# A hybrid RWKV-7 / HGRN2 block: two transposes moved from TensorE to VectorE and DMA, HGRN2 units overlapped, TensorE's durations re-estimated

## The chip, the cores and the metric

The kernel runs on one core of a Trainium2 chip, as one program in one launch. The metric is the device time of one execution in microseconds; the median of several executions is compared. All data are float32. Five engines work side by side, each on its own queue of instructions in order: TensorE (PE, with its weight load PEld), VectorE (DVE), ScalarE (ACT), GpSimd (POOL) and SyncE (SP), which here only issues DMAs. ScalarE issues some DMAs too. TensorE writes to PSUM; the other data lie in SBUF (128 partitions) or in DRAM.

## The reference, cut to what matters

One layer of a trunk block over 1024 tokens of width 1024. The change touches the first third, the token mixing:

```python
u = rmsnorm(h, norm_mix_g)
cols = u @ w_in                       # [RWKV-7 columns | HGRN2 columns | gate_a | gate_b]
y_a = rwkv7_branch(rw_cols, ...)      # 16 heads of 64: a delta-rule state per head, GroupNorm, bonus, gate g
y_b = hgrn2_branch(hg_cols, ...)      # 8 heads of 128: gated linear recurrence in chunks of 64 tokens
h = h + (sigmoid(gate_a) * y_a + sigmoid(gate_b) * y_b) @ w_out
# then cross-attention into 256 memory tokens, a SwiGLU feed-forward layer, a last RMSNorm
```

RWKV-7, per token: `state = state * w + (state @ a) b^T + v k^T`, `o = state @ r`; then GroupNorm per head, `* ln_w + ln_b`, plus a bonus term, times a gate g. HGRN2, per chunk of 64 tokens: `b = cumsum(log f)`, `scores[t,s] = sum_k q[t,k] exp(b[t,k] - b[s,k]) k[s,k]` for s up to t, `o = scores @ i + (q exp(b)) @ state`, and the state is carried on.

## The kernel before

**Stages.** `rw_prep` (up to about 400 us) projects the RWKV-7 columns and writes the chunk factors AR, BK, V and the gate g to DRAM. `mixing` (400 to 1300 us) runs the RWKV-7 recurrence, the HGRN2 branch, the rest of the projection and the merge. Attention and the feed-forward layer follow. Only `mixing` and the planner class `Pace` change.

**The order in mixing.** The order of all engines' instructions is fixed at build time by a planner. Every piece of work is a generator (`job`, `bkt`, `values`, `merge`, `hgrn`, `level`, `blocks`, `state`, `ev_*`, `weights`, ...). It yields the engine it wants next, the tiles that must be ready, the room that must be free in a ring of buffers, a condition and a priority. `Pace` keeps a clock for each engine, and `Pace.note` adds an estimated duration for each instruction; `Pace.matmul` (L172 to L184) estimates TensorE's: something for a change of form (`took`, L177), 0.109 for a transpose, `0.0155 + 0.000417 * cols` for a float32r product, and by columns for a float32 one (L184). The loop at L1615 resumes what is due by these clocks. TensorE's default work is `project()`: 768 steps ("slots") of three matmuls of 512 columns, the HGRN2 and gate columns of w_in, float32 split in two float32r halves. Between two other pieces of work at least RUN = 3 slots are put, if any are due. The estimates set only the order; on the chip engines wait by semaphores.

**RWKV-7 jobs.** There are 16 jobs (`job(n)`), one for 8 heads and 128 tokens, two chunks of 64, one each PERIOD = 41 slots at the earliest. Job n loads AR and BK (128 partitions x 8 x 128), multiplies them (psc), inverts a triangular matrix in blocks of 16 and 32 (Aq, Tq, UD, pu, py) and then does two steps of the recurrence: `cm<-Z,AR`, R, `cm<-R,U`, Z, `cm<-Z,BKT`, `po<-Z,SR`. `bkt(n, BK)` (L836) makes BKT, in which each of BK's eight 128x128 blocks is transposed: two groups of four TensorE transposes into PSUM (pbk), each copied to SBUF by ScalarE. BK's buffer is free (`locks.remove("BK")`) after the second. After the recurrence, the job normalizes po into xc (128 tokens-in-chunk and head parity x 8 x 64), multiplies by ln_w, adds zb (ln_b and bonus, from DRAM), and writes xc to `yad`, tokens by features, in four DMAs of 64 KB with runs of 256 bytes (L1090 to L1094).

**The merge.** When four jobs have written a half of the tokens and the gates are there, `merge(j, h)` (L1131) loads one 128-feature strip of yad by tokens (mya, in `tok3` order), turns it with four TensorE transposes (pya), multiplies it on VectorE by sigmoid(gate_a) * g (msa, from DRAM) and adds the HGRN2 side (msb), and the sum goes to y_d. For the last strip, j = 7, `last_gates` (L1289) does the product ahead (gya). `turned` counts strips turned; the key projections of attention, at the end of `project()`, wait until all 16 are (L1583).

**HGRN2 units.** `hgrn(j, h)` (L1424) is one head and 512 tokens, 16 in all. It starts when the unit before has issued its output (`hstate["done"]`, L1426), then starts `blocks` (factors within 4 tokens), `level` for 8, 16 and later 32 and 4, and `state` (L1376: eb, kh, qe, pkh, pSh, and the chain of states Sh). TensorE makes scores psB, psA, psl, which VectorE merges into one tile `sc`, and then the output poh. The flag "free" is set when the last level's factors reach TensorE (L1470).

Of the kernel before, what the change touches and what calls it, by code (L numbers as in the profile page):

```python
# [10 lines left out]
F32 = mybir.dt.float32  # L11
# [21 lines left out]
class Pace:  # L33
# [138 lines left out]
    def matmul(self, aps, op):  # L172
# [4 lines left out]
        took = 0.11 if form != self.form else 0.0  # L177
# [6 lines left out]
        return took + max(0.02, 0.00173 * cols / min(2 if rows == outs == 64 else 4, 128 // rows * 128 // outs))  # L184
# [3 lines left out]
def tile_trunk(ctx, tc, x, mem, norm_mix_g, w_in, rw_mu, rw_w0, rw_w2, rw_a0, rw_a2, rw_g2,  # L188
# [153 lines left out]
    def scratch(name, shape):  # L342
        return dram.tile(shape, F32, name=name)
# [7 lines left out]
    yad = scratch("ya_d", [S, D])  # L351
# [380 lines left out]
    def mixing(mctx):  # L732
# [50 lines left out]
        def pe(*tiles, **kw):  # L783
            return on("PE", *tiles, **kw)
# [51 lines left out]
        def bkt(n, BK):  # L836

            BKT = BKTs[n] = jp.tile([P, 8, P], F32, tag="BKT", name="BKT")
            for q in range(2):
                yield pe(BK, room=W1)  # L840
                pbk = pw.tile([P, 4, P], F32, tag="w", name="pbk")
                for e in range(4):
                    nc.tensor.transpose(pbk[:, e, :], BK[:, 4 * q + e, :], ident)
                pace.hold(pbk)
                yield on("ACT", pbk, prio=-1)
                nc.scalar.activation(BKT[:, 4 * q:4 * q + 4, :], pbk, AF.Copy)
                pace.drop(pbk)
            locks.remove("BK")

# [7 lines left out]
        def job(n):  # L857
# [146 lines left out]
            for c in range(2):  # L1004
# [31 lines left out]
                yield pe(Z, BKTs[n], prio=-2, cond=lambda: c == 0 or last or n + 1 in states)  # L1036
# [51 lines left out]
            nc.gpsimd.tensor_tensor(xf, xf, zb, op=ALU.add)  # L1088
            locks.remove("zb")
            yield on("SP", xc)  # L1090
            ys = yad[i * P:(i + 1) * P, j0 * P:(j0 + 4) * P].rearrange("(c t) (j q v) -> q c t j v", c=2, j=4, q=2)
            for hh in range(2):
                for c in range(2):
                    nc.sync.dma_start(out=ys[hh, c], in_=x4[H[hh], :, c, :])  # L1094
# [17 lines left out]
        turned = [0]  # L1112
# [18 lines left out]
        def merge(j, h):  # L1131
# [20 lines left out]
            ya = t(0, [P, 4, P], "mya")  # L1152
            nc.sync.dma_start(out=ya, in_=tok3(yad, h, j * P, P))
# [3 lines left out]
            yield pe(ya, room=W1, prio=1)  # L1157
            pt = pw.tile([P, 4, P], F32, tag="w", name="pya")
            for i in range(4):
                nc.tensor.transpose(pt[:, i, :], ya[:, i, :], ident)  # L1160
            pace.drop(ya)
            turned[0] += 1
            if pool is fp:
                locks.discard("zb")
            pace.hold(pt)
            yield on("DVE", pt, y, prio=-1)
            nc.vector.tensor_tensor(y, pt.rearrange("p i t -> p (i t)"), y, op=ALU.mult)
            pace.drop(pt)
# [120 lines left out]
        def last_gates():  # L1289
# [5 lines left out]
            ya = [jp.tile([P, 4, P], F32, tag="BS", name="mya") for _ in range(NHALF)]  # L1295
            nc.sync.dma_start(out=g, in_=gd[j].rearrange("h p t -> p h t"))
            for h in range(NHALF):
                nc.sync.dma_start(out=ya[h], in_=tok3(yad, h, j * P, P))
            for h in range(NHALF):
                yield pe(ya[h], room=W1, prio=1)  # L1300
                pt = pace.hold(pw.tile([P, 4, P], F32, tag="w", name="pya"))
                for i in range(4):
                    nc.tensor.transpose(pt[:, i, :], ya[h][:, i, :], ident)
                yield on("DVE", pt, g, prio=-1)
                nc.vector.tensor_tensor(g[:, h, :], pt.rearrange("p i t -> p (i t)"), g[:, h, :], op=ALU.mult)
                pace.drop(pt)
                flags.add(("gya", h))
                turned[0] += 1
# [67 lines left out]
        def state(j, h, M):  # L1376
# [8 lines left out]
            yield on("POOL", eb, q)  # L1385
# [38 lines left out]
        def hgrn(j, h):  # L1424

            yield pe(cond=lambda: hstate.get("done", 0) == NHALF * j + h  # L1426
# [918 lines left out]
```

## Time and profile before

| | us |
|---|---|
| median of 3 runs | 2315.07 (2314.65 to 2315.83) |
| profiled execution | 2322.77 |
| its span, first to last instruction | 2321.1 |

| mixing stage, instructions by group | count | mean ns |
|---|---|---|
| TensorE pbk<-ident,BK (transposes) | 128 | 281 |
| TensorE pya<-ident,mya (transposes) | 64 | 277 |
| ScalarE BKT<-pbk, 128x512 | 32 | 595 |
| VectorE msa<-pya,msa, 128x512 | 14 | 690 |
| VectorE UD<-TD, 32x32 transposes of 128x256 | 16 | 446 |

A group's mean is the time of one instruction from start to end. TensorE's instructions overlap in its pipeline, so means and busy times of TensorE are larger than the time from one start to the next. Idle time of an engine counts only where the engine sets the pace. "A <- B" in a wait list: an instruction of tile A waited for one that writes or reads tile B. PEclk is the share of TensorE's clock that was granted.

### The profile page before, as it was taken

How to read it: one execution, taken by the hardware profiler on the slowest of the kernel's cores; microseconds unless marked ns; L12 is line 12 of the kernel's file. 1: busy time of each engine (PE TensorE's matmuls, PEld its weight loads, DVE VectorE, ACT ScalarE, POOL GpSimd, SP SyncE). 2: the span in 40 equal slices, each digit the busy share in tenths (PEclk: the TensorE clock that was granted, in tenths of full speed). 3: DMA queues.
4: the chain of work that ended last, by engine and by line, in shares of the span. 5: the costliest groups of instructions: out<-in, count | busy, mean ns of one | idle time of the engine just before them, and what ended most of it. 6: DMA issues, size and time to landing. Idle time of an engine off the chain costs nothing.

```text
span 2321.1 us, 46517 instructions
## 1 busy us (share of the span) xinstructions
PE 2266.5 (98%) x18006; PEld 1845.9 (80%) x18006; DVE 1528.3 (66%) x2510; ACT 1134.9 (49%) x2214; POOL 1027.7 (44%) x1109
## 2 busy tenths in 40 slices
PE   7999999999999999999999999999999999999998
PEld 5788887778878877778787788888878888888887
DVE  5788884656676766875757466555768675566655
ACT  6545454465666655556665424443453333334533
POOL 3655555554565655665656100000266655551212
PEclk9999999999999999999999999999999999999999
DMA  5444445334435345445333897117933423248653
GB/s 173 124 128 125 126 125 172 76 89 98 99 95 135 81 107 130 126 97 128 90 98 102 279 353 261 55 55 267 287 112 118 129 91 117 93 160 303 206 173 118
DMA packets 424666, 331.06 MB, mean 143 GB/s; under 512 B 140619, under 2 KB 349629, under 8 KB 423037
## 3 DMA queue, kind: packets, MB, share of 16 engines
q1 hardware_dynamic: 353405, 313.93, 44.1%
q10 hardware_dynamic: 69696, 9.44, 2.8%
q0 software_dynamic: 1344, 4.72, 0.5%
q8 instruction: 142, 2.33, 0.4%
q14 instruction: 79, 0.65, 0.1%
HBM read 228.12 MB, written 99.35 MB: 141 GB/s over the span
## 4 chain that ended last, share of the span: by engine, by line
PE 69%; DMA 5%; DVE 4%; POOL 3%; issue 2%; ACT 2%; SPq 0%; ACTq 0%; POOLq 0%; DVEq 0%
PE pproj L103 19%; PE P L304 6%; PE P L303 6%; PE P L305 6%; PE acc L304 3%; PE acc L305 2%; PE acc L303 2%; PE cm L103 2%; PE pw L305 2%; PE pw L303 2%; PE pw L304 2%; PE poh L103 1%; PE pq L304 1%; PE pq L303 1%; PE pq L305 1%
## 5 line engine op out<-in xcount | busy, mean ns | idle before, releaser
L103 PE MATMUL pproj<-uh,whi 128*128 128x512 f32 x768 | 321.8, 419 | 3.7 <-ACT sa L103 1.4
L103 PE MATMUL pproj<-ul,whi 128*128 128x512 f32 x768 | 302.7, 394 | 1.8 <-issue 1.8
L103 PE MATMUL pproj<-uh,wlo 128*128 128x512 f32 x768 | 302.6, 394 | 0.0
L289 POOL TENSOR_TENSOR wl<-wraw,wh 128x512 fp32r<-128x512 f32 x87 | 120.6, 1392 | 204.8 <-ACT wh L285 171.6
L303 PE MATMUL pproj<-uh,whi 128*128 128x512 f32 (+1 forms) x432 | 177.5, 411 | 1.0 <-ACT uh L331 0.7
L285 ACT ACTIVATE whi<-wraw 128x512 fp32r<-128x512 f32 (+1 forms) x166 | 100.9, 618 | 158.4 <-PE pw L305 73.7
L103 POOL TENSOR_TENSOR wlo<-wraw,whi 128x512 fp32r<-128x512 f32 x96 | 129.3, 1355 | 105.3 <-ACT whi L103 95.5
L103 PEld LDWEIGHTS pproj<-uh,whi 128*128 128x128 f32 x768 | 145.3, 189 | 38.3 <-DVE q L103 2.0
L103 PEld LDWEIGHTS pproj<-ul,whi 128*128 128x128 f32 x768 | 145.4, 189 | 35.0 <-issue 2.2
L305 PE MATMUL pproj<-uh,wlo 128*128 128x512 f32 (+1 forms) x432 | 170.4, 394 | 1.8 <-POOL wlo L289 1.8
L304 PE MATMUL pproj<-ul,whi 128*128 128x512 f32 (+1 forms) x432 | 170.4, 395 | 0.0
L103 PEld LDWEIGHTS pproj<-uh,wlo 128*128 128x128 f32 x768 | 145.8, 190 | 24.9
L280 POOL TENSOR_TENSOR ss<-ss,nhalf 128x4 f32<-128x4 f32 (+1 forms) x7 | 6.2, 883 | 324.6 <-DVE ss L279 205.6
L103 ACT ACT_TABLE_LOAD x102 | 130.9, 1283 | 18.5 <-issue 6.0
L289 POOL TENSOR_TENSOR wlT<-wraw,whT 128x512 fp32r<-128x512 f32 x72 | 101.0, 1412 | 84.9 <-ACT whT L285 67.0
L285 ACT ACTIVATE wh<-wraw 128x512 fp32r<-128x512 f32 x143 | 87.1, 624 | 97.0 <-PE P L304 69.0
L289 DVE TENSOR_TENSOR wlo<-wraw,whi 128x512 fp32r<-128x512 f32 x134 | 93.5, 706 | 56.1 <-ACT whi L285 54.8
L304 PE MATMUL acc<-wl,th 128*128 128x512 f32 x308 | 119.9, 389 | 0.1
L303 PE MATMUL acc<-wh,th 128*128 128x512 f32 x308 | 119.8, 389 | 0.0
L305 PE MATMUL acc<-wh,tl 128*128 128x512 f32 x308 | 119.8, 389 | 0.0
L2289 DVE TENSOR_TENSOR tl<-tl,th 128x512 fp32r<-128x512 f32 x77 | 60.4, 796 | 62.5 <-ACT th L2288 58.8
L303 PE MATMUL pw<-whi,ah 128*128 128x512 f32 x256 | 100.6, 393 | 0.6 <-ACT ah L285 0.6
(456 smaller groups left out, 6277.2 us busy)
## 6 DMA issues: line engine op xcount, KB each, us to landing
wraw<-in_w_in_dram SPq DMA_DIRECT2D x148, 256.0 KB
wraw<-in_ffn_w_dram SPq DMA_DIRECT2D x145, 256.0 KB
y<-in_ffn_w_dram SPq DMA_DIRECT2D x22, 512.0 KB
wsum_d<-y SPq DMA_DIRECT2D x11, 1024.0 KB
hsum_d<-s SPq DMA_DIRECT2D x44, 256.0 KB
tl<-hsum_d SPq DMA_DIRECT2D x44, 256.0 KB
wraw<-wsum_d SPq DMA_DIRECT2D x44, 256.0 KB
hid_d<-s SPq DMA_DIRECT2D x33, 256.0 KB
```

The lines of the kernel that those rows point to most:

```text
L103: r = getattr(self.engine, op)(*a, **kw)
L280: nc.gpsimd.tensor_tensor(dst, tmp, nhalf[:, 0:n], op=ALU.pow)
L285: nc.scalar.activation(hi, src, AF.Copy)
L289: e.tensor_tensor(lo, src, hi.bitcast(F32), op=ALU.subtract)
L303: nc.tensor.matmul(ps, ah, bh, start=first, stop=False)
L304: nc.tensor.matmul(ps, ah, bl, start=False, stop=False)
L305: nc.tensor.matmul(ps, al, bh, start=False, stop=last)
L2289: tt(hl, hl.bitcast(F32), hh.bitcast(F32), op=ALU.subtract)
```

## The change

- **BKT.** `bkt` now transposes BK on VectorE in one instruction, in 32x32 blocks within each partition quarter, into the tile BKT. Four DMAs of 128 KB, one for each quarter of partitions, write it to a scratch tensor BKd in DRAM in runs of 128 bytes, and one DMA of 512 KB reads it back into BKT in runs of 512 bytes, so that each block lands in place. BK's lock is released after the VectorE instruction. The flag ("BKT", n) tells the third product of the recurrence that it may be planned.
- **RWKV-7 results.** xc is turned in 32x32 blocks on VectorE into zb, and four DMAs from zb write `yad`, which now is features by tokens, in runs of 256 bytes. `merge` and `last_gates` load a strip with two DMAs in runs of 2 KB (`load_ya`), and `gated` multiplies it by the gate in two instructions of 256 columns on VectorE or GpSimd, by whichever the planner has free. TensorE's pya and the `turned` count are gone; the key projections no longer wait for it.
- **HGRN2 units.** A unit starts when the one before has given its last level's factors to TensorE (`begun`). Its psB and its eb product wait for the earlier unit's output (`done`) as before.
- **Estimates.** In `Pace.matmul`, a change to a float32r form is taken as 0.15 instead of 0.11, a column of a float32 product as 0.0019 instead of 0.00173, at least 0.024 instead of 0.02.

```diff
@@ -174,14 +174,14 @@
         cols = math.prod(right.shape[1:])
         rows, outs = (next(t for t in (32, 64, 128) if t >= n) for n in (right.shape[0], math.prod(left.shape[1:])))
         form = rows, outs, right.dtype
-        took = 0.11 if form != self.form else 0.0
+        took = 0.0 if form == self.form else 0.15 if right.dtype == F32R else 0.11
         self.form = form
         if op == "transpose":
             return took + 0.109
         if right.dtype == F32R:
             return took + 0.0155 + 0.000417 * cols
 
-        return took + max(0.02, 0.00173 * cols / min(2 if rows == outs == 64 else 4, 128 // rows * 128 // outs))
+        return took + max(0.024, 0.0019 * cols / min(2 if rows == outs == 64 else 4, 128 // rows * 128 // outs))
 
 
 @with_exitstack
@@ -348,7 +348,7 @@
     vd_ = scratch("v_d", [S, D])
     zd = scratch("z_d", [2, S // P, P, HALF])
     gd = scratch("g_d", [KT, NHALF, P, HALF])
-    yad = scratch("ya_d", [S, D])
+    yad = scratch("ya_d", [2, 2, 2, 4, 32, S])
     sad = scratch("sa_d", [KT, NHALF, P, HALF])
     sbd = scratch("sb_d", [KT, NHALF, P, HALF])
     NM = mem.shape[1]
@@ -835,17 +835,19 @@
 
         def bkt(n, BK):
 
-            BKT = BKTs[n] = jp.tile([P, 8, P], F32, tag="BKT", name="BKT")
-            for q in range(2):
-                yield pe(BK, room=W1)
-                pbk = pw.tile([P, 4, P], F32, tag="w", name="pbk")
-                for e in range(4):
-                    nc.tensor.transpose(pbk[:, e, :], BK[:, 4 * q + e, :], ident)
-                pace.hold(pbk)
-                yield on("ACT", pbk, prio=-1)
-                nc.scalar.activation(BKT[:, 4 * q:4 * q + 4, :], pbk, AF.Copy)
-                pace.drop(pbk)
+            yield on("DVE", BK)
+            BKT = BKTs[n] = pace.hold(jp.tile([P, 8, P], F32, tag="BKT", name="BKT"))
+            nc.vector.transpose(BKT.rearrange("p e t -> p (e t)"), BK.rearrange("p e t -> p (e t)"))
             locks.remove("BK")
+            BKd = pace.scratch(dram, [32, 32, P], tag="BKd", bufs=2)
+            yield on("SP", BKT)
+            for q in range(4):
+                nc.sync.dma_start(out=BKd[:, :, 32 * q:32 * q + 32].rearrange("m t f -> t m f"),
+                                  in_=BKT[32 * q:32 * q + 32].rearrange("p e (b f) -> p (e b) f", f=32))
+            yield on("SP", BKd)
+            nc.sync.dma_start(out=BKT, in_=BKd.rearrange("(e b) t f -> (b t) e f", b=4))
+            pace.drop(BKT)
+            flags.add(("BKT", n))
 
         DIAG = 16 * 64 + 16
 
@@ -1033,7 +1035,7 @@
                 for hh in range(2):
                     nc.scalar.activation(Z[H[hh], c::2, hh, :], pa[H[hh]], AF.Copy)
                 steps[n] += 1
-                yield pe(Z, BKTs[n], prio=-2, cond=lambda: c == 0 or last or n + 1 in states)
+                yield pe(Z, BKTs[n], prio=-2, cond=lambda: ("BKT", n) in flags and (c == 0 or last or n + 1 in states))
                 if not last:
                     for jj in range(4):
                         for hh in range(2):
@@ -1086,12 +1088,14 @@
             nc.gpsimd.tensor_tensor(x4, x4, lnw.unsqueeze(2).to_broadcast([P, 4, 2, 64]), op=ALU.mult)
             yield on("POOL", zb)
             nc.gpsimd.tensor_tensor(xf, xf, zb, op=ALU.add)
+            yield on("DVE", zb, xc)
+            nc.vector.transpose(zb, xc.rearrange("p m (b v) -> p b m v", b=2))
+            yield on("SP", zb)
+            for hh in range(2):
+                for b in range(2):
+                    nc.sync.dma_start(out=yad[hh, j0 // 4, :, :, :, i * P + 64 * b:i * P + 64 * b + 64].rearrange("b j v t -> v (b j) t"),
+                                      in_=zb[64 * hh + 32 * b:64 * hh + 32 * b + 32].rearrange("v (m t) -> v m t", t=64))
             locks.remove("zb")
-            yield on("SP", xc)
-            ys = yad[i * P:(i + 1) * P, j0 * P:(j0 + 4) * P].rearrange("(c t) (j q v) -> q c t j v", c=2, j=4, q=2)
-            for hh in range(2):
-                for c in range(2):
-                    nc.sync.dma_start(out=ys[hh, c], in_=x4[H[hh], :, c, :])
             flags.add(("gn", n))
             if i % 4 == 3:
                 for j in range(j0, j0 + 4):
@@ -1109,7 +1113,15 @@
 
         parts = {}
 
-        turned = [0]
+        def gated(out, ya, g):
+
+            for c in range(2):
+                t = lambda ap: ap.rearrange("p (i c b t) -> p i c b t", i=4, c=2, b=2)[:, :, c]
+                either(0.5).tensor_tensor(t(out), ya.rearrange("p (i b c t) -> p i b c t", i=4, b=2, c=2)[:, :, :, c], t(g), op=ALU.mult)
+
+        def load_ya(t, j, h):
+            for hh in range(2):
+                nc.sync.dma_start(out=t[H[hh]], in_=yad[hh, j // 4, :, j % 4, :, h * HALF:(h + 1) * HALF])
 
         def ready(j, h, what):
             d = parts.setdefault((j, h), set())
@@ -1149,23 +1161,16 @@
                          cond=lambda: not {"merge", "zb"} & locks)
                 locks.update(("merge", "zb"))
             t = lambda n, shape, name: pace.hold(pool.tile(shape, F32, tag=tags[n], name=name, bufs=bufs))
-            ya = t(0, [P, 4, P], "mya")
-            nc.sync.dma_start(out=ya, in_=tok3(yad, h, j * P, P))
+            ya = t(0, [P, HALF], "mya")
+            load_ya(ya, j, h)
             y, yb = t(1, [P, HALF], "msa"), t(2, [P, HALF], "msb")
             nc.sync.dma_start(out=y, in_=sad[j, h])
             nc.sync.dma_start(out=yb, in_=sbd[j, h])
-            yield pe(ya, room=W1, prio=1)
-            pt = pw.tile([P, 4, P], F32, tag="w", name="pya")
-            for i in range(4):
-                nc.tensor.transpose(pt[:, i, :], ya[:, i, :], ident)
+            yield on("DVE", ya, y)
+            gated(y, ya, y)
             pace.drop(ya)
-            turned[0] += 1
             if pool is fp:
                 locks.discard("zb")
-            pace.hold(pt)
-            yield on("DVE", pt, y, prio=-1)
-            nc.vector.tensor_tensor(y, pt.rearrange("p i t -> p (i t)"), y, op=ALU.mult)
-            pace.drop(pt)
             yield on("POOL", y, yb)
             either(1.0).tensor_tensor(y, y, yb, op=ALU.add)
             pace.drop(yb)
@@ -1292,20 +1297,14 @@
             yield on("SP", yad, room=((fp, "BK", 1), (jp, "BS", 2)),
                      cond=lambda: steps[NJ - 1] >= 6 and all("a" in parts.get((j, h), ()) for h in range(NHALF)))
             g = kept["g"] = fp.tile([P, NHALF, HALF], F32, tag="BK", name="gya")
-            ya = [jp.tile([P, 4, P], F32, tag="BS", name="mya") for _ in range(NHALF)]
+            ya = [jp.tile([P, HALF], F32, tag="BS", name="mya") for _ in range(NHALF)]
             nc.sync.dma_start(out=g, in_=gd[j].rearrange("h p t -> p h t"))
             for h in range(NHALF):
-                nc.sync.dma_start(out=ya[h], in_=tok3(yad, h, j * P, P))
+                load_ya(ya[h], j, h)
             for h in range(NHALF):
-                yield pe(ya[h], room=W1, prio=1)
-                pt = pace.hold(pw.tile([P, 4, P], F32, tag="w", name="pya"))
-                for i in range(4):
-                    nc.tensor.transpose(pt[:, i, :], ya[h][:, i, :], ident)
-                yield on("DVE", pt, g, prio=-1)
-                nc.vector.tensor_tensor(g[:, h, :], pt.rearrange("p i t -> p (i t)"), g[:, h, :], op=ALU.mult)
-                pace.drop(pt)
+                yield on("DVE", ya[h], g, prio=-1)
+                gated(g[:, h, :], ya[h], g[:, h, :])
                 flags.add(("gya", h))
-                turned[0] += 1
 
         mT = []
 
@@ -1382,7 +1381,7 @@
             act(eb, b, AF.Exp)
             either(0.7).tensor_tensor(kh.rearrange("p (n t) -> p n t", t=C), b8[:, :, C - 1:C].to_broadcast([P, NC, C]), b8,
                                       op=ALU.subtract)
-            yield on("POOL", eb, q)
+            yield on("POOL", eb, q, cond=lambda: hstate.get("done", 0) == NHALF * j + h)
             el = gp.tile([P, NC], F32, tag="el", name="el", bufs=2)
             nc.gpsimd.tensor_copy(el, eb[:, C - 1::C])
             M["qe"] = gp.tile([P, HALF], F32, tag="qe", name="qe")
@@ -1423,7 +1422,8 @@
 
         def hgrn(j, h):
 
-            yield pe(cond=lambda: hstate.get("done", 0) == NHALF * j + h
+            done = lambda: hstate.get("done", 0) == NHALF * j + h
+            yield pe(cond=lambda: hstate.get("begun", 0) == NHALF * j + h
                      and all((n, j, h) in flags for n in ("b", "q", "1-f")))
             M = {}
             start(blocks(j, h, M))
@@ -1441,7 +1441,7 @@
                 nc.vector.copy_predicated(sc, mk[m].unsqueeze(1).to_broadcast([P, 4, C]), ps)
                 pace.drop(ps)
 
-            yield pe(cond=lambda: ("m", j, h, 0) in flags)
+            yield pe(cond=lambda: ("m", j, h, 0) in flags and done())
             qb, kb = M["qb"], M["kb"]
             yield pe(qb, kb, room=W1)
             psB = scores("psB", kb, qb)
@@ -1468,6 +1468,7 @@
             yield pe(cond=lambda: ("m", j, h, 4) in flags)
             yield pe(M[4], room=W1)
             flags.add(("free", j, h))
+            hstate["begun"] = NHALF * j + h + 1
             psl = scores("psl", M[4], M[4])
             pace.drop(M[4])
             yield on("DVE", psl, prio=-1)
@@ -1580,7 +1581,7 @@
             if k0 == 0:
                 room = pace.space(pp, "proj", 1)
                 if room is None or max(pace.ready(t) for t in w) > now or room > now or \
-                        h is None and ("mem" not in flags or j >= KEYS - 2 and turned[0] < NU * NHALF or max(pace.ready(t) for t in mT) > now):
+                        h is None and ("mem" not in flags or max(pace.ready(t) for t in mT) > now):
                     return False
                 if at == begin[c] and c + 2 < NW:
                     start(weights(c + 2))
```

## The prediction

> **What bounds the kernel now.** I read the page first, then busy time by stage, then TensorE's waits, then single instructions in the timeline.
>
> ```profile
> span 2321.1 us, 46517 instructions
> PE 2266.5 (98%) x18006; PEld 1845.9 (80%) x18006; DVE 1528.3 (66%) x2510; ACT 1134.9 (49%) x2214; POOL 1027.7 (44%) x1109
> ```
>
> ```profile
> 400.00:500.00 100.00, 90.83 (x1134) 72.13 (x1133) 60.07 (x124) 55.81 (x94) 55.27 (x80) 0.97 0.34 82
> ...
> 1200.00:1300.00 100.00, 95.51 (x816) 77.73 (x814) 56.57 (x89) 43.57 (x98) 58.34 (x53) 0.98 0.44 136
> sum 900.00, PE 876.73 PEld 704.41 DVE 589.30 ACT 511.34 POOL 517.03; mean PE 97.41 PEld 78.27 DVE 65.48 ACT 56.82 POOL 57.45
> ```
>
> The window rows give start:end, length, the busy time of PE, PEld, DVE, ACT and POOL, then granted clock, DMA share and GB/s. The change touches the mixing stage alone, 400 to 1300 us. In it PE is busy for 876.73 of 900 us, so 23.3 us are idle; DVE has 65%, ACT and POOL 57%. So the stage is bound by the sum of what TensorE must issue, and what TensorE no longer issues comes off the time, unless a new wait fills the hole. TensorE's present waits there, longest first:
>
> ```profile
> PE pkh L103 <- DVE kh L103: 4.9, 1, 4.9
> PE poh L103 <- DVE sc L103: 2.9, 1, 2.9
> PE cm L103 <- DVE Z L103: 2.5, 3, 1.2
> ...
> PE pproj L103 <- ACT sa L103: 1.4, 1, 1.4
> ...
> PE pu L103 <- ACT BKT L103: 0.7, 1, 0.7
> ```
>
> Columns: total us, times, longest. Most are operands that came late once or twice. No row of this list is a wait for a weight of pproj (whi, wlo).
>
> **Part 1: TensorE's transposes go.** The groups first, then one group between projections (start, length).
>
> ```profile
> L103 PE MATMUL pbk<-ident,BK 128*128 128x128 f32 x128 | 20.3, 281 | 0.3 <-DVE SR L103 0.3
> L103 PE MATMUL pya<-ident,mya 128*128 128x128 f32 x64 | 9.9, 277 | 0.7 <-DMA mya<-ya_d 0.7
> ```
>
> ```profile
> 406.44 0.39 PE L103 MATMUL pproj<-ul,whi 128*128 128x512 f32 x1
> 406.67 0.60 PE L103 MATMUL pbk<-ident,BK 128*128 128x128 f32 x4
> 407.02 0.48 PE L103 MATMUL pproj<-uh,whi 128*128 128x512 f32 x1
> 407.34 0.40 PE L103 MATMUL pproj<-uh,wlo 128*128 128x512 f32 x1
> ```
>
> They are 128 + 64 transposes in fours: 48 groups. Their busy time, 20.3 + 9.9 = 30.2 us, overlaps with the neighbours, so it is too much. What counts is from start to start: a projection matmul takes 0.23 us (406.44 to 406.67). From the first transpose to the second projection matmul behind it are 407.34 - 406.67 = 0.67 us, in which one projection matmul (0.23) was got done. So a group costs 0.44 us. 48 x 0.44 = 21.1 us.
>
> One of the 48 is worth nothing. It is the last pya, at 1292 us, behind the last projection of the stage:
>
> ```profile
> 1291.61 2.07 ACTq L1702 DMA_DIRECT2D wraw<-in_xa_wv_dram  x4
> 1298.28 0.63 ACT L285 ACTIVATE whi<-wraw 128x512 fp32r<-128x512 f32 x1 [3.96 <-DMA wraw<-in_xa_wv_dram]
> ```
>
> There the next stage's first weights are only fetched from 1291.61 on and are there at 1298.28, whatever TensorE does between. That leaves 47 x 0.44 = 20.7 us. With the transposes go the waits that were theirs or their eviction's: pu for ACT's BKT 0.7 and, in the group rows, pbk's 0.3, 1.0 us together; pya's 0.7 there is the one at 1292 and counts nothing. After that, the projection's own evictions (the row "pproj <- ACT sa") are what is late next.
>
> **Part 2: the same work on VectorE, ScalarE and GpSimd.**
>
> ```profile
> L103 DVE STREAM_TRANSPOSE UD<-TD 128x256 f32<-128x256 f32 x16 | 7.1, 446 | 0.6
> L103 DVE TENSOR_REDUCE Tq<-pr 128x2 f32<-128x4 f32 x16 | 2.5, 157 | 0.5
> L103 DVE TENSOR_TENSOR msa<-pya,msa 128x512 f32<-128x512 f32 x14 | 9.7, 690 | 6.0 <-PE pya L103 5.7
> L103 DVE TENSOR_TENSOR SR<-psc,keep 128x256 f32<-128x256 f32 x64 | 26.6, 415 | 0.5
> L103 DVE TENSOR_TENSOR m<-m,k 128x256 f32<-128x256 f32 x40 | 31.3, 793 | 21.2 <-ACT m L103 21.0
> L103 ACT ACTIVATE BKT<-pbk 128x512 f32<-128x512 f32 x32 | 19.0, 595 | 23.3 <-PE pbk L103 10.6 <-DMA Aq<-Ad 3.6 <-DMA Ad<-BS 3.0
> ```
>
> A 32x32 transpose of 256 columns takes 0.446 us; the smallest VectorE instruction, 0.157 us, stands for its fixed part. So (0.446 - 0.157)/256 = 1.13 ns a column: 1.31 us for BK's 1024 columns, 0.74 us for the 512 of a result tile; in proportion, without a fixed part, 1.78 and 0.89 us, which I keep as the upper end. 16 x (1.31 + 0.74) = 32.8 us. The product with the gate was 0.69 us x 16 = 11.0 us, one operand from PSUM. It becomes two instructions of 256 columns with both operands in SBUF; such pieces take from 0.415 us (one operand in PSUM) to 0.793 us (both in SBUF, beside GpSimd). I take 0.70: 32 x 0.70 = 22.4 us, if VectorE gets all. VectorE: 32.8 + 22.4 - 11.0 = +44 us, 589 to 633 us of the stage's 900. ScalarE loses 32 x 0.595 = 19 us. VectorE at 70% is no bound, but it works in order: whatever waits behind a transpose is later by 1.3 us. TensorE's longest waits for VectorE, the first three rows of its list (4.9 + 2.9 + 2.5 us), grow by 1 us in proportion to its load, 44/589. The gate products wait on VectorE for the landing that pya waited for on TensorE; behind them waits VectorE's whole queue, the recurrence's sums too. I take +1, and keep 0 and +16 as ends (below).
>
> **Part 3: the way through DRAM.** BKT is now written in four DMAs with 128-byte pieces and read back in one, by SP.
>
> ```profile
> q1 hardware_dynamic: 133821, 83.87, 34.0%
> q10 hardware_dynamic: 69471, 9.05, 7.1%
> g_d<-gt POOLq DMA_DIRECT2D x8, 512.0 KB, 6.5
> 646.51 2.58 SPq L103 DMA_DIRECT2D ya_d<-xc  x4
> SPq L103 <- POOL wlo L103: 302.8, 70, 19.5
> 524.29 0.59 ACT L103 ACTIVATE BKT<-pbk 128x512 f32<-128x512 f32 x1
> 570.55 0.69 PE L103 MATMUL cm<-Z,BKT 128*64 128x64 f32 x16
> ```
>
> The queue rows hold packets, MB and the share of 16 engines over 400 to 1300 us. q10: 0.071 x 16 x 900 us / 69471 = 14.7 ns for a packet of 130 bytes; q1: 36.6 ns for one of 627 bytes. BK is 512 KB: 4096 packets out, 4096 x 14.7/16 = 3.8 us, and 1024 packets of 512 bytes back, 2.3 us. Four issues on SP take 2.58 us, and a DMA of 512 KB lands 6.5 us after its issue in the row of g_d. So 1.3 (transpose) + 2.6 + 2 x 6.5: BKT is there some 17 us after BK. The tightest place in the trace is the third job: BKT complete at 524.9, first used at 570.55, 46 us later. Twice 17 us would still be hidden, so this part costs 0. (If the cover went, each microsecond beyond it would be one of TensorE's idle time, up to 16 times.) SP issues 5 DMAs a job and one for each gate load more: 96 x 0.65 = 62 us of 900. The reading DMA waits on SP for the writing one, and behind it wait weight loads, the next BK and Z. But SP itself stands for 302.8 us waiting to be allowed the next weight load (70 times, up to 19.5 us), and TensorE never waited for weights; 6 us more, once a job, fit in. The result tiles are transposed before they are written, so their DMAs wait for VectorE in place of GpSimd; they are read 2 KB at a time in place of 512 bytes. Nothing on TensorE is behind them except the last gates, and that is in the hidden end.
>
> [...] If each piece cost what a 627-byte one does, the write would be 9.4 us in place of 3.8, still within the 46, and the sum the same.
>
> **Part 4: HGRN2 units overlap; estimates.** The next unit's exponentials may begin when the last unit's last factor is used, not when its output is issued. No TensorE work goes. What may go is idle time in front of pkh, poh, psA, and the slow clock behind it:
>
> ```profile
> 427.85 1.09 PE L103 MATMUL pkh<-ident,kh 128*128 128x128 f32 x4 [4.86 <-DVE kh L103]
> 500.17 0.49 PE L103 MATMUL pproj<-ul,whi 128*128 128x512 f32 x1 [1.81 <-issue]
> 426.00:432.00 6.00, 4.15 (x12) 3.52 (x13) 5.73 (x13) 3.37 (x5) 4.75 (x5) 0.50 0.56 131
> 500.00:507.00 7.00, 6.83 (x55) 5.63 (x56) 3.27 (x10) 3.54 (x18) 0.00 (x0) 0.55 0.24 78
> ```
>
> The 4.86 us belong to the first unit, which has none before it: they stay. The 2.9 us in front of poh lie in the last but one; the clock of 1200 to 1300 us is 0.98, so 2 us more hang on it. Of these 4.9 I take 3. The new estimates (0.15 for 0.11 after a change of form, 0.0019 for 0.00173 a column) change only the order written at build time. I cost them at 0: they shift other engines' work by some 0.1 us against TensorE's per group, to either side; the idle 23.3 us is what they could gain at most, and as much the loss that I allow.
>
> Behind both gaps the clock is half, 0.50 and 0.55. [...]
>
> **Sum.** -20.7 - 1.0 - 3 + 1 = -23.7 us. The profiled execution took 2322.77 us, 1.7 us more than its span and 0.3% more than the median of 2315.07; the difference applies to either. 2315.07 - 23.7 = **2291 us**.
>
> **Rivals.**
> 1. *More waits go.* Most of the 23.3 us of idle time and of the lost clock (0.97 and 0.98 of 100 us in the two windows shown, 5 us) goes, as units overlap and the transposes' PSUM tiles are free for others: 60% of 28 is 17 us in place of 4 - 1, 2277. For it: most waits are for operands just late. Against: several are of the recurrence or of issue, which nothing here moves.
> 2. *Given back to VectorE.* VectorE is 44 us fuller and in order, and "cm <- DVE Z" is a wait of 0.8 us each time (2.5 in 3). If 20 of the stage's 32 state steps meet it, that is 16 us: 2307. For it: the overlap puts a second unit's pieces in front of the recurrence. Against: VectorE keeps 30% free.
> 3. *Slower.* The overlap moves work of the next unit on VectorE and GpSimd ahead of what TensorE needs now, and stalls like the one at 427.85 arise in the middle units. One costs 4.9 us plus the half clock until 432 (0.5 x 4.2 = 2.1 us): 7 us. From four of them on the kernel is slower; with five, 2315 - 24 + 35 = 2326. Against: pieces are ordered by when they are due, and VectorE and GpSimd share the load.
> 4. *The overlap does nothing*, since a unit waits for its projections anyway: 2294, inside the forecast's own spread.
>
> **How the numbers follow.** The forecast, with rival 4, has 0.55 (2284 to 2299); rival 1 has 0.15, rival 2 has 0.18, rival 3 has 0.12. A measurement of this kernel can tell 0.2%, 4.6 us, from no change: 2310.4 to 2319.7. Rival 2 reaches into it with 0.08 of its chance. So faster 0.80, same 0.08, slower 0.12. The range 2274 to 2312 leaves out rival 3, the end of rival 2 and a little below rival 1.
>
> **What would show it.** In the mixing stage no pbk or pya; a projection matmul every 0.23 us in their place; the next stage's first weights fetched at about 1268 instead of 1291.61. STREAM_TRANSPOSE groups of 1.2 to 1.8 and 0.7 to 0.9 us; VectorE at 68 to 71%. Wrong: TensorE waits for BKT, for weights, or idle time above 30 us in the stage; a write of BK that takes over 30 us; a stage that is shorter by the 21 us with an attention stage longer by as much.

## The result and the profile after

The changed kernel takes 2353.02 us (median, 2352.13 to 2353.78); the kernel before, run beside it, 2315.45 us. The ratio is 1.0168, 95% interval 1.0156 to 1.0180: slower by 1.7%, where 2291 us, faster by 1%, was predicted. The profiled execution took 2352.13 us. That of the kernel before took 2322.77, some 7 us over its median; so the stages below show 29.3 of the 37.6 us of loss, and the rows of the kernel before may hold some 7 us too much, at a place that is not known (in the third stretch most other kernels here have 972 to 977 us).

The page's head, after. TensorE is busy for 9 us less than before, and the span is 29.3 us longer:

```profile
span 2350.4 us, 46264 instructions
PE 2257.4 (96%) x17814; PEld 1832.8 (78%) x17814; DVE 1572.8 (67%) x2566; ACT 1119.6 (48%) x2178; POOL 1026.3 (44%) x1107
...
PEclk9999999999999999999998789999999999999999
```

The clock row has its hole in the 22nd to 24th of 40 slices of 58.8 us, deepest from 1293 to 1352 us, behind mixing. So I cut the span in three: from the first to the last projection matmul of mixing; from there to the first matmul of attention's w_out (pw), which I call attention's start; the rest. Busy time by stage, before (columns as in the prediction):

```profile
381.30:1291.20 909.90, 887.86 (x11638) 712.04 (x11636) 589.75 (x1227) 520.99 (x1140) 521.28 (x576) 0.99 0.42 108
1291.20:1342.70 51.50, 48.11 (x294) 41.26 (x293) 30.77 (x51) 25.68 (x47) 4.78 (x6) 1.00 0.97 326
1342.70:2321.10 978.40, 966.20 (x4406) 799.18 (x4404) 617.66 (x887) 384.94 (x717) 304.76 (x225) 0.99 0.51 170
```

The same three stretches, after:

```profile
381.00:1264.20 883.20, 866.17 (x11446) 688.46 (x11445) 623.50 (x1272) 504.99 (x1104) 508.47 (x565) 1.00 0.52 124
1264.20:1371.90 107.70, 61.60 (x294) 52.55 (x292) 45.24 (x72) 31.49 (x57) 14.96 (x15) 0.74 0.66 205
1371.90:2350.40 978.50, 965.68 (x4404) 798.75 (x4404) 613.93 (x878) 379.99 (x707) 306.16 (x225) 1.00 0.51 169
```

Mixing became 26.7 us shorter (909.9 to 883.2), near the 23.7 forecast, though not by the same terms (Part 1 below). Attention's start, with the same 294 matmuls, became 56.2 us longer (51.5 to 107.7). The rest is the same. Of the 107.7 us TensorE is idle for 46.1, and the granted clock is 0.74: some 56 us of the stretch at half clock (2 x 0.26 x 107.7). About half of these, 27.5 us, lie in the idle time; the other 28.7 cost some 14 us. So the 56.2 us are some 43 of idle time (46.1, before 3.4) and some 14 of half clock.

What stands there? All engines' waits from 1264 to 1372 us, after:

```profile
POOL msa L103 <- DMA msa<-sa_d: 59.6, 5, 12.7
DVE wlo L289 <- ACT whi L285: 35.4, 8, 9.6
ACT whi L285 <- DMA wraw<-in_xa_wv_dram: 23.9, 8, 10.4
ACT sa L103 <- DMA mya<-ya_d: 19.8, 1, 19.8
ACT whi L285 <- DMA wraw<-in_xa_wk_dram: 19.0, 3, 10.7
PEld pproj L103 <- ACT sa L103: 17.2, 1, 17.2
PE pproj L103 <- ACT sa L103: 17.0, 1, 17.0
```

`msa` and `mya` are tiles of the merge. SyncE's DMA issues that touch the merge, before and then after (a merge loads msa from sa_d, and at its end writes y_d):

```profile
1279.07 0.32 SPq L103 DMA_DIRECT2D msa<-sa_d  x1
...
1285.77 0.32 SPq L103 DMA_DIRECT2D y_d<-msa  x1
...
1289.81 0.56 SPq L103 DMA_DIRECT2D msa<-sa_d  x1
...
1298.74 0.41 SPq L103 DMA_DIRECT2D y_d<-msa  x1
```

```profile
1274.43 0.32 SPq L103 DMA_DIRECT2D msa<-sa_d  x1
...
1293.42 0.33 SPq L103 DMA_DIRECT2D y_d<-msa  x1
...
1294.97 0.47 SPq L1684 DMA_DIRECT2D wraw<-in_xa_wk_dram  x1
1297.27 0.33 SPq L103 DMA_DIRECT2D msa<-sa_d  x1
...
1298.17 1.41 SPq L1684 DMA_DIRECT2D wraw<-in_xa_wk_dram  x3
1307.93 0.34 SPq L103 DMA_DIRECT2D y_d<-msa  x1
...
1322.93 0.34 SPq L103 DMA_DIRECT2D y_d<-msa  x1
...
1337.26 0.33 SPq L103 DMA_DIRECT2D y_d<-msa  x1
...
1350.86 0.34 SPq L103 DMA_DIRECT2D y_d<-msa  x1
...
1353.26 12.12 SPq L1849 DMA_DIRECT2D yraw<-y_d  x16
```

Before, the last merge is loaded 1.4 us before the last projection (1291.2). After, five of the 14 merges are loaded behind it (1264.2), one at a time, 13 to 15 us from one y_d to the next, and in one in-order queue with attention's weights (wraw). Most of that is the merge's wait for its own load, 59.6 us in five times by the first row above. w_out reads y_d, so it cannot begin before 1353. A second thing stands in the same stretch. ScalarE's issues, and the matmuls that wait behind them, after:

```profile
1269.22 14.51 ACTq L1703 DMA_DIRECT2D wraw<-in_xa_wv_dram  x4
1283.77 0.60 ACT L103 ACTIVATE sa<-pproj 128x512 f32<-128x512 f32 x1 [19.80 <-DMA mya<-ya_d]
```

```profile
1284.42 0.80 PE L103 MATMUL pproj<-mT,wkey 128*128 128x256 f32 x2 [16.98 <-ACT sa L103]
```

Attention's first weight buffers lie over those of the merge. ScalarE's four issues stand for 14.5 us until a merge lets go of them, ScalarE's eviction of a projection stands behind them, and TensorE behind that for 17 us. Of TensorE's other 29 us of idle time, 18 are waits for attention's own weights (whi, wlo), which come by the same queues, and the last 11 lie directly before w_out.

### The profile page after: what moved, and what is told of

Its sections match the earlier page's. It is cut to its first block, busy times and chain, and to the rows that moved or that the text cites. A ratio compares the mean times of both kernels' runs of the same rounds, so it can differ in the third digit from the quotient of the medians.

```text
span 2350.4 us, 46264 instructions
## 1 busy us (share of the span) xinstructions
PE 2257.4 (96%) x17814; PEld 1832.8 (78%) x17814; DVE 1572.8 (67%) x2566; ACT 1119.6 (48%) x2178; POOL 1026.3 (44%) x1107
```

## The experiments

Where do the late merges come from? In the planner every DMA has a price, by the length of its runs, on one common clock, and an issue of SyncE is planned for no earlier than the landing of the eighth DMA before it:

```python
start = max(start, self.landings[-8] if e == "SP" else 0.0, self.read.get(aps[0].name, 0.0))
run = min(x.ap[-1][1] * 4 if x.ap[-1][0] == 1 else 4 for x in aps)
rate = 180e3 if run >= 1024 else 130e3 if run >= 512 else 80e3 if run >= 256 else 50e3
```

BK's 128-byte runs fall into the last class: 524288 bytes at 50 KB/us are 10.5 us for each of 16 jobs. In the trace, the 4096 packets of a job (median 13 ns each) are done in 3.9 to 6.6 us. Three theories:

- **A.** The planner takes BK's writes as too slow. In its clock the landings of the results come late, so it puts merges late, and the chip follows that order.
- **B.** The key projections no longer wait for the merges' transposes, so they and attention's loads come too early and collide with the merges.
- **C.** The overlap of HGRN2 units fills VectorE and GpSimd, and the merges get no turn.

**1. The planner's rate alone.** The changed kernel, with the same instructions in another order:

```diff
-  rate = ... 80e3 if run >= 256 else 50e3
+  rate = ... 80e3 if run >= 256 else 130e3 if run >= 128 else 50e3
```

> The changed kernel; in the planner alone, the estimated DMA rate of pieces of 128 to 255 bytes is 130 KB/us instead of 50. Theory A (backlog): the planner takes BK's write for 10.5 us where the trace has 4 to 5, so merges come due late, 7 of 14 are left when the projection ends and run one after another, 14 us each, in SP's queue between attention's loads. Then at most 2 merges are left, attention's TensorE stalls fall from some 50 us to under 10, and the time is 2285 to 2300 us. Theory B (the key projections no longer wait for the merges, so attention begins too early) and theory C (the overlap of HGRN2 units): the time stays at 2340 or more.

2307.54 us beside 2312.57 before, ratio 0.9985 (0.9976 to 0.9995). Busy time by stage, mixing and attention's start:

```profile
380.10:1272.30 892.20, 869.46 (x11446) 693.90 (x11445) 631.65 (x1271) 499.60 (x1097) 536.56 (x583) 0.99 0.52 128
1272.30:1330.40 58.10, 50.90 (x294) 45.01 (x292) 33.62 (x56) 25.83 (x47) 5.76 (x7) 0.91 0.90 294
```

Attention's start falls from 107.7 to 58.1 us, with one merge behind the last projection in place of five. For A. (The expectation speaks of 7 late merges in the changed kernel; its trace has five.) But mixing takes 892.2 in place of 883.2: another order costs 9 us there, and the time missed A's range by 7.5. That A's chain runs by the landings is read from the planner's code; the planner's clock itself was not recorded.

**2. No backlog at all.** Six merges (strips 4 to 6, both halves) are left out: loads, gate product and sum, so this kernel's result lacks them.

```diff
+  SKIP = ((4, 0), (5, 0), (6, 0), (4, 1), (5, 1), (6, 1))
+  if what == "b" and (j, h) in SKIP: nc.sync.dma_start(out=yd[j, h], in_=t)   # in spill
+  if (j, h) in SKIP: return                                                   # in merge
```

> The changed kernel without six merges, (4,0), (5,0), (6,0), (4,1), (5,1), (6,1): their strips of y_d get the HGRN2 side alone, written when it is spilled; loads, gate product and sum of those strips are left out. Theory A (the merges that are left over hold attention's first loads and its w_out product): from the last projection to w_out's first matmul there are 52 to 58 us as before, not 107.7, and the time is 2295 to 2303 us. Theory B (attention and the key projections begin too early) and C (overlap): 2340 or more, since all else is as changed.

2305.46 us beside 2313.76, ratio 0.9963 (0.9950 to 0.9976). Attention's start:

```profile
1275.90:1325.40 49.50, 47.42 (x294) 41.33 (x293) 30.70 (x50) 26.14 (x47) 4.82 (x6) 1.00 0.94 326
```

With no merge left behind the last projection, attention's start is 49.5 us, even 2 less than before, at full clock. So the 56 us are the backlog's, idle time and half clock together. The time is 2.5 us over A's range, since mixing is 895.8 us in this order.

**3. The key projections wait for all 14 merges.** The wait that B misses, put back in the changed kernel and made stricter:

```diff
-  h is None and ("mem" not in flags or max(...) > now)
+  h is None and ("mem" not in flags or j >= KEYS - 2 and merged[0] < (NU - 1) * NHALF or max(...) > now)
```

> The changed kernel with the key projections waiting until all 14 merges are done. Theory B: the loss goes, about 2291. Theory A: the merges are as late as before and the keys come after them, so 2350 or more; nothing is gained.

2373.07 us, ratio 1.0248 (1.0232 to 1.0265): 20 us worse than the changed kernel. Five merges are behind the last projection as in the changed kernel, and attention's start is 128.1 us. B falls: the wait makes no merge earlier, it only keeps back what TensorE could do meanwhile.

**4. One part undone, three kernels.** From the changed kernel: BK by TensorE again (no_bkt); the results by TensorE again, with the wait on `turned` (no_ya); units without overlap (no_hg). The first two are those parts of the diff above, read backward; the third is:

```diff
-  yield pe(cond=lambda: hstate.get("begun", 0) == NHALF * j + h     # no_hg
+  yield pe(cond=lambda: hstate.get("done", 0) == NHALF * j + h
```

> The changed kernel with BK turned by TensorE as before; results, overlap and estimates as changed. Theory A: without BK's long DMA in the planner's clock few merges are left at the end; 16 groups of transposes at 0.44 us are still saved: 2300 to 2312 us. Theories B and C: 2335 or more, since results, keys and overlap are still as changed.

> The changed kernel with the RWKV results turned by TensorE as before and the key projections waiting for them; BK, overlap and estimates as changed. Theory A: zb is free sooner but BK's estimate stays, so 1 to 3 merges are left: 2295 to 2315 us. Theory B: the keys wait again, so 2295 to 2305. Theory C: 2335 or more.

> The changed kernel without the overlap of HGRN2 units. Theory A: the backlog stays (BK's estimate and zb are as changed), 5 or more merges are left, 2335 to 2360 us. Theory C: the loss goes, 2285 to 2300 us. Theory B: 2335 or more.

- no_bkt: 2329.56 us, 1.0087 (1.0066 to 1.0108). Attention's start 61.0 us with one merge in it: the backlog goes with BK's write, as A says. But the time missed all three theories' numbers. Mixing is 908.8 us: BK's transposes are back on TensorE, and idle time (28.2 us) and half clock (20.5 us) with them.
- no_ya: 2306.47 us, 0.9979 (0.9968 to 0.9989). Attention's start 65.1 us, one merge in it, though BK's price is still 10.5 us. So the price alone does not make the backlog; the new way of the results, whose DMAs hold the buffer `zb` until they have landed, is needed too.
- no_hg: 2336.65 us, 1.0109 (1.0094 to 1.0124). Four merges are still late (A had 5 or more), attention's start is 91.5 us. C falls as the cause, though the overlap adds to it: without it the changed kernel is 16 us faster (2336.65 beside 2353.02).

TensorE's new estimates were not undone in the changed kernel, so what they add to the backlog is not shown.

**5. One part alone on the kernel before, four kernels.** The overlap (only_hg), the results (only_ya) and BK (only_bkt) are those parts of the diff above; only_est is the two lines of `Pace.matmul`, the second as in the diff:

```diff
-  took = 0.11 if form != self.form else 0.0                                      # only_est
+  took = 0.0 if form == self.form else 0.15 if right.dtype == F32R else 0.11
```

> The kernel before with the overlap of HGRN2 units alone. The prediction's part 4 had 3 us for it: 2308 to 2312 beside 2312 to 2315 for before. Theory C: slower by more than 10 us. Theory A: no backlog, since neither BK's DMA nor zb is changed, so no loss.

> The kernel before with the RWKV results turned by VectorE and DMA alone (with it the key projections no longer wait for the merges). Theory A: zb is held longer, but without BK's DMA in the planner's clock no merge is left over; 16 groups of 0.44 us go, one of them worth nothing: 2304 to 2309 beside a before of 2313. Theory B (the keys no longer waiting makes attention begin too early): more than 50 us from the last projection to w_out plus 20, so 2325 or more.

> The kernel before with BK turned by VectorE and DMA alone. 32 groups of 0.44 us go from TensorE, 14 us. Theory A: BK's estimated 10.5 us in the planner's DMA clock alone push merges back, 2 or more to the end: from the last projection to w_out 60 to 80 us instead of 51, so 2308 to 2328. If only zb makes the backlog: 2298 to 2302.

> The kernel before with TensorE's new estimated durations alone. The prediction's part 4: 0, with ends at either side: 2308 to 2318 beside a before of 2313. If the estimates alone change how the merges fall: beyond 2320.

only_hg: 2306.59 us, 0.9969 (0.9959 to 0.9980). only_ya: 2331.22 us, 1.0072 (1.0057 to 1.0087). only_bkt: 2337.71 us, 1.0101 (1.0082 to 1.0120). only_est: 2307.28 us, 0.9965 (0.9953 to 0.9977). The overlap and the estimates each gain alone; each of the two moved transposes, alone, makes the kernel slower, though it takes work off TensorE. All four missed their ranges: only_hg and only_est came out 1.4 and 0.7 us below, only_ya and only_bkt 22 and 10 us above. The time of only_ya is one that B had named, but not its place: attention's start is 61.0 us, not over 70, and no merge is late. By length, attention's start has 9.5 us of only_ya's loss and 14.8 of only_bkt's (61.0 and 66.3 us; in only_bkt TensorE waits 13.0 there for a merge's mya). Mixing is only 4.3 and 5.9 us longer than before, but it holds 6.6 and 13.3 us less work ("net" in the table below); so there some 11 and 19 us more are lost to idle time and half clock. TensorE's longest waits in mixing, only_ya and then only_bkt:

```profile
PE pkh L103 <- DVE kh L103: 8.0, 3, 4.9
PE pyb L103 <- DVE yn L103: 4.5, 1, 4.5
```

```profile
PE psB L103 <- DVE kb L103: 8.1, 1, 8.1
PE pkh L103 <- POOL kh L103: 6.1, 1, 6.1
```

They are operands of HGRN2 and of a normalization that came late once to three times; the one of 4.9 us for kh is in the kernel before as well. No BKT is among them.

**6. The rate, and jobs closer together.** With A's repair the recurrence may start earlier, so that merges end earlier: `PERIOD` is 39 or 37 slots in place of 41.

```diff
-  PERIOD = 41
+  PERIOD = 37
```

> a_rate130 with PERIOD 39 instead of 41, so each RWKV job may begin two slots earlier than the one before allows, the last some 30 slots. Theory A': what a_rate130 still lacks against 2291 are the last three merges, which wait for the last job and run one after another; with jobs earlier they end with the projection: last projection to w_out 52 to 54 us instead of 58, time 2290 to 2302. If they are not the limit: 2305 to 2310 like a_rate130.

> a_rate130 with PERIOD 37. Theory A': merges end before the projection does; last projection to w_out at most 53 us, time 2287 to 2300. If earlier jobs only crowd VectorE: more idle time in the mixing stage (over 30 us) and 2305 or more.

39: 2316.40 us, 1.0012 (0.9999 to 1.0024), above both of its ranges. 37: 2292.98 us, ratio 0.9914 (0.9896 to 0.9931), as A' says, the fastest of all and faster than both kernels. Busy time by stage at 37:

```profile
381.00:1269.10 888.10, 868.81 (x11445) 691.37 (x11444) 614.55 (x1254) 504.56 (x1105) 543.41 (x596) 0.99 0.53 130
1269.10:1319.10 50.00, 47.38 (x295) 41.48 (x294) 31.43 (x54) 26.66 (x52) 4.55 (x6) 1.00 0.95 328
```

Now both are had: mixing 21.8 us shorter than before, attention's start 50.0 us. But 39, with the same instructions, has no backlog either (52.2 us) and loses 20 us in mixing: 34.2 us idle and 34.1 us at half clock. Why 37 is good and 39 is not was not found.

All kernels in one table, from the traces. "Net" is mixing's length less TensorE's idle time in it, less half of its time at half clock: what its instructions cost at full clock. Merges: loaded behind the last projection.

| kernel | mixing | idle | half clock | net | attention's start | merges |
|---|---|---|---|---|---|---|
| before | 909.9 | 22.0 | 20.5 | 879.0 | 51.5 | 0 |
| after | 883.2 | 17.0 | 6.8 | 862.9 | 107.7 | 5 |
| a_rate130 | 892.2 | 22.7 | 23.9 | 858.4 | 58.1 | 1 |
| a_skip | 895.8 | 26.9 | 13.7 | 862.3 | 49.5 | 0 |
| a_keys | 885.0 | 17.9 | 10.2 | 862.9 | 128.1 | 5 |
| no_bkt | 908.8 | 28.2 | 20.5 | 871.2 | 61.0 | 1 |
| no_ya | 883.9 | 14.6 | 3.4 | 867.6 | 65.1 | 1 |
| no_hg | 888.3 | 22.8 | 20.5 | 856.3 | 91.5 | 4 |
| only_hg | 899.4 | 15.6 | 6.8 | 880.4 | 51.8 | 0 |
| only_ya | 914.2 | 29.1 | 30.7 | 872.4 | 61.0 | 0 |
| only_bkt | 915.8 | 35.0 | 41.0 | 865.7 | 66.3 | 1 |
| only_est | 901.3 | 16.2 | 13.7 | 878.8 | 48.8 | 0 |
| r_p39 | 908.3 | 34.2 | 34.1 | 857.8 | 52.2 | 0 |
| r_p37 | 888.1 | 19.3 | 17.1 | 860.4 | 50.0 | 0 |

(Half-clock time that lies in idle time is counted once, as idle. So the columns do not add up to the last unit. Each row is one profiled execution; those of before and only_bkt were 6 to 7 us over their medians.)

## Why the prediction was wrong

**The step that failed** is in Part 3: "Nothing on TensorE is behind them except the last gates, and that is in the hidden end." "They" are the results' DMAs. Behind them are the merges; behind the merges is y_d, and behind y_d all of w_out; and beside them in SyncE's queue and in the same buffers are attention's first loads. Before, the last merge was loaded 1.4 us ahead of the last projection. That was the room there was, and I never read it off. Experiment 2 prices the step: attention's start is 49.5 us without the late merges and 107.7 with them, the whole 2305.46 and 2353.02. The prediction named this outcome as what would make it wrong ("with an attention stage longer by as much"), but gave it no mechanism, no price and no chance.

**Why they came late** is a step that I didn't take: in Part 4 the estimates were weighed only for TensorE, not the planner's DMA rate, which the new 128-byte runs make 10.5 us for about 4 to 5. Experiment 1 shows that this rate alone decides some 50 of the 56 us; no_ya shows that it does so only together with the results' new way. How much of that is the held `zb` and how much the landings was not measured by itself, nor what the new estimates add to it.

**Part 1 was right in size.** Its 21.1 us were 32 + 16 groups of 0.44. Alone, the results take 6.6 us off the net (879.0 to 872.4) where 15 groups give 6.6, and BK takes 13.3 (to 865.7) where 32 give 14.1. In the changed kernel it is 16.1 of the 20.7 forecast, with the rate 20.6, without the overlap (no_hg) 22.7: the order of the rest moves it by some 4 us either way of the 19.9 that the two gave alone. That mixing as a whole came near the forecast is partly luck. The missing 4.6 us were made up by idle time and half clock, which fell by 10.6 where 3 were counted. And the same instructions in other orders (a_rate130, a_keys, r_p37, r_p39) have mixing at 885.0 to 908.3 us. The first weights of attention were forecast at about 1268 us; their first issue begins at 1269.22, but the four take until 1283.73.

**Part 2 was right.** After, the new instructions on VectorE and the gate product on GpSimd:

```profile
L103 DVE STREAM_TRANSPOSE BKT<-BK 128x1024 f32<-128x1024 f32 x16 | 19.7, 1229 | 0.1
L103 DVE STREAM_TRANSPOSE zb<-xc 128x512 f32<-128x512 f32 x16 | 11.1, 694 | 0.1
...
L103 DVE TENSOR_TENSOR msa<-mya,msa 128x256 f32<-128x256 f32 x7 | 3.5, 500 | 6.0 <-DMA msa<-sa_d 6.0
```

```profile
L103 POOL TENSOR_TENSOR msa<-mya,msa 128x256 f32<-128x256 f32 x9 | 7.2, 808 | 16.7 <-DMA msb<-sb_d 8.5 <-DMA msa<-sa_d 8.2
```

1.23 and 0.69 us were forecast as 1.31 and 0.74, the gate product's 0.50 and 0.81 as 0.70. VectorE gained 33.8 us of mixing (589.75 to 623.50), 44 forecast. Of the 32 gate products, 12 lie behind mixing with the late merges and GpSimd took 9 of the other 20; some 7 us of the gain are other work that the planner gave to VectorE in this order. Rival 2, that the gain is given back to VectorE, did not come in the changed kernel: "cm <- DVE Z" is 1.8 us in two waits, before 2.5 in three.

**Part 3's BKT was hidden, as it said, but with less room.** The first and last of its steps, after (count, ns, first and last start):

```profile
L103 SPq DMA_DIRECT2D BKd<-BKT x64: 325/642/4700, 413.9 to 1133.7; - x64
L103 DVE STREAM_TRANSPOSE BKT<-BK x16: 1224/1226/1245, 406.1 to 1130.7; 128x1024 f32<-128x1024 f32 x16
L103 SPq DMA_DIRECT2D BKT<-BKd x16: 382/482/1348, 422.8 to 1142.2; - x16
```

In the first job 16.7 us lie between transpose and reading DMA, in the last 11.5, over all 16 from 6.7 to 25.8. BKT was forecast there some 17 us after BK; in 7 of the 16 jobs the read was not even issued by then. Nor was the cover 46 us: in the kernel before, the tightest job is not the third but the eleventh, with BKT complete at 925.15 and first used at 962.46, 37 us later. The cover held all the same: the read is issued 31.3 us or more ahead of its first use, and TensorE waits for BKT nowhere. For weights (wlo) it waits 1.1 us in mixing, in two times, where Part 3 had none. Of the two prices that I weighed, 3.8 us for the write by the 130-byte packets' row and 9.4 if small pieces cost what large ones do, the trace has about 4 to 5. The planner's own 10.5 us was on neither side of it: I priced the transfer on the chip, and not in the program that orders the work.

**Part 4, the overlap.** Forecast -3 us, alone -0.31% (0.2 to 0.4), some 7 us: idle time 22.0 to 15.6 and half clock 20.5 to 6.8 (upper ends, as the profile of before is of a slower execution than its median). The mechanism was right, the size too small. Rival 3, that the overlap makes the kernel slower by stalls in mixing, did not come: alone the overlap gains (only_hg), and in the changed kernel mixing is 5 us shorter with it than without (no_hg). That the whole is 16 us slower with it comes from attention's start. The estimates, costed at 0, gained 0.35%, 8 us, inside the bound of 23.3 that I gave.

**The rivals** all looked for the loss inside mixing. The one that ended on the slower side had the wrong part (the overlap) and the wrong place. What stays open: why only_ya and only_bkt lose 7 to 13 us of idle time and 10 to 20 us at half clock within mixing, where all parts together, in the changed kernel, lose none. Over all kernels the order moves mixing's idle time between 14.6 and 35.0 us, without a rule that I found.

## What to carry to other kernels

Where a build-time planner sets the order, an operation of a new kind has two prices, the chip's and the planner's; a DMA shape that falls into the planner's worst class moves work that has nothing to do with it, so look up its class before you call it hidden. When the bounding stage gets shorter, read off what is left to do at its end and how much room there was (here 1.4 us): background work that was just in time becomes the next stage's start. And undo each part as well as try it alone: here the work that each part took off TensorE was priced about right, and the loss lay in the order that the planner made of the rest.

## What the runs showed of the hardware

After, a short packet took less time than a longer one, though a byte in it cost more: a 128-byte packet from SBUF to DRAM took 13 ns (median of 65536), near the 14.7 that the prediction worked out from a queue with 130 bytes a packet on average, and a 512-byte packet 27 ns (median of all in the trace), so that a byte cost about twice as much in the short ones (0.10 and 0.05 ns). The 512 KB of a job were still written in 4.4 us (median of 16, 3.9 to 6.6), some 119 KB/us.

In these traces the clock's halving doesn't go by the gap's length alone. Two gaps of TensorE, after:

```profile
868.68 1.05 PE L103 MATMUL py<-T,BS 16*32 16x16 f32 x64 [4.04 <-DMA T<-Td]
...
1112.61 0.69 PE L103 MATMUL psB<-qb,kb 128*64 128x64 f32 x16 [2.20 <-POOL kb L103]
```

After 4.04 us the clock is half, after 2.20 it stays full, while the prediction's row has it at about half after 1.81. What tells them apart is where the gap lies. In the 14 traces every stretch at half clock begins on one grid of 3.41 us in its trace, and lasts whole steps of it (but for the one that the end of the execution cuts off): after, the starts at 868.56 and 1271.33 us are 118 steps of 3.413 us apart; the half-clock column above holds multiples of 3.41. The steps of the grid that hold the two gaps, each with the stretch behind it, after; and the step with the gap of 1.81, before:

```profile
865.15:868.56 3.41, 0.00 (x0) 0.00 (x0) 2.38 (x4) 3.35 (x5) 1.14 (x2) 1.00 0.32 104
868.56:875.39 6.83, 6.71 (x78) 5.45 (x79) 2.79 (x5) 4.70 (x20) 3.87 (x3) 0.50 0.04 15
1110.91:1114.32 3.41, 1.71 (x21) 1.47 (x22) 3.16 (x9) 1.78 (x10) 3.41 (x4) 1.00 0.08 19
1114.32:1117.74 3.42, 3.42 (x72) 2.89 (x72) 3.15 (x11) 0.60 (x1) 3.15 (x5) 1.00 0.66 166
```

```profile
497.30:500.71 3.41, 1.60 (x13) 0.85 (x13) 2.71 (x7) 0.56 (x2) 1.27 (x1) 1.00 0.18 53
```

Counted over all 14 traces, from mixing to 15 us before the end, by TensorE's busy share of a step at full clock: below 30% the next step is at half clock in 43 of 43 cases, from 65% on in none of 7643, and between them in 39 of 85 (before and after alone: 7 of 7, none of 1085, 5 of 13). The 1.81 us lie whole in one step and are a little over half of it; of the 2.20 us, 1.70 lie in one step. So a gap of about half a step halved the clock in one of these two cases and left it in the other.

In attention's start, after, the half clock came on top of the waits, but much of it lay within them: 46 us of idle time, and 56 us at half clock, of which some 28 outside the idle time cost some 14.
